# Two encoder layers on one core: Fourier transforms folded twice, value products in runs of six, and roots by Newton steps

## Chip, cores and metric

One core of a Trainium2 chip runs the whole program. The metric is device time in microseconds (us), the median of several runs. The profile comes from one execution that was recorded.

## What is computed

```python
def reference(x, norm1, w_in, w_fourier, b_fourier, q_norm, k_norm, sink, ...):
    for l in range(DEPTH):                       # 2 layers, 512 positions, 1024 channels
        h = rmsnorm(x, norm1[l])
        p = h @ w_in[l]                          # u (512) | q (8 x 64) | k (2 x 64) | v (2 x 64)
        ...
        y_f = fourier_mix(u, w_fourier[l], b_fourier[l])   # Re(FFT2 over positions, channels) @ W_f + b
        q = rope(rmsnorm(q, q_norm[l]))
        k = rope(rmsnorm(k, k_norm[l]))
        y_a = windowed_gqa(q, k, v, sink[l])     # |i-j| <= 128, softmax with a sink
        mix = jnp.concatenate([rmsnorm(y_f, ...), rmsnorm(y_a, ...)], axis=-1)
        x = x + mix @ w_o[l]
        h = rmsnorm(x, norm2[l])
        up = dwconv_centred(h @ w_up[l], conv_w[l], conv_b[l])
        x = x + (jax.nn.silu(gate) * val) @ w_down[l]
    return x
```

All of it is float32 to the outside.

## The kernel before, in words

x lies as eight tiles of 128 channels x 512 positions. A product of matrices is made in one of two ways (`mm3`, L114): plain f32, one matmul instruction that the profile shows as two records on TensorE (L118); or, where both factors were split into a high and a low fp32r part (`split`, L98: ScalarE makes the high part, VectorE the low one), three matmuls high-high, low-high and high-low (L120 to L122). The FFN, q, k, v and W_o go the second way; layer 0's Fourier group goes in plain f32, layer 1's in three fp32r products.

A layer goes as follows. The root of the norm (`col_rstd`, `row_rstd`, `rsqrt`, L206) ends in `rb`, which ScalarE copies (L226). The q, k, v product has two groups: group 1 (q3, k, v) and group 0 (q0 to q2). `fold_h` (L400) multiplies a tile of x by its norm (one SCALAR_TENSOR_TENSOR, "stt") and folds it over positions: `fold` (L329) writes the sum of position n and 512-n (257 columns) and the difference (255 columns), with one COPY of two columns and two TENSOR_TENSOR of 255. The weight W_u is folded over channels in the same way (`fold_wu`, L335). The **u-stage** (L551) multiplies the eight folded tiles by the eight folded weights: for each tile five products of 258 or 256 columns, into three banks `pee` and one `poo`. `stage_out` (L580) and `tail_out` (L570) copy the four blocks (cosine and sine parts of positions and of channels) out of PSUM. Then two DFT **stages** (L594): stage 0 over channels, stage 1 over positions, each thirteen products in plain f32, or 36 matmuls in fp32r, of 256 or 258 columns, against the tables `tabs` and `alts` from `load_tables` (L275). W_f (L620) and its norm follow.

`prep` (L429) makes the roots of q and k (`rsqrt` with n=16 for k and q3, n=24 for q0 to q2) and their rotation. The power itself is one GpSimd instruction (L210, tiles `qk2r`, `qk3r`). `turn_q` and `turn_k` (L473, L483) transpose them on TensorE. `attention` (L500) goes by pairs of heads, 3, 0, 1, 2, in two halves of two query blocks: scores (L517), a reduction on VectorE (L521), the exponential on ScalarE, a scaling on GpSimd (L526), transposes on TensorE (L529), copies on ScalarE (L531), and six value products per half (L536) of 128 rows by 64 columns into the upper or lower half of one bank:

```python
for j in ((0, 1, 2), (1, 2, 3))[half]:
    ...
    for e in range(2):
        nc.tensor.matmul(py[64 * e:64 * e + 64, ...], vp[:, j, ...], pT[:, half, e, ...], ...)
```

The products of W_o's first half are spread between the attention's steps by `issue_after`. W_o's second half and the FFN follow; while layer 0's FFN runs, `presplit` (L149) folds and splits layer 1's weights on ScalarE and VectorE and stores them in DRAM (`kept`).

The order of instructions on each engine is not the code's: the tile framework's scheduler sets it, by its own estimate of when inputs are ready and by free buffers (`TEMPS`, `BANKS`). A change in one place so moves instructions in others.

Of the kernel before, what the change touches and what calls it, by code (L numbers as in the profile page):

```python
# [37 lines left out]
def encoder_kernel(tc, t):  # L38
# [236 lines left out]
    def load_tables(l):  # L275


        rows = t["dft"].rearrange("i p c -> (i p) c")[:, 257:]
        tab = []
        for i in range(2):  # L280
            raw = temp(512, "m4") if l else cp.tile([P, 512], F32, tag=f"th{i}", name=nm("tab"))
            nc.sync.dma_start(raw[:, :257], t["dft"][i, :, :257])
            if i == 0:
                nc.vector.memset(raw[:1, 257:512], 0.0)
                nc.sync.dma_start(raw[1:16, 257:512], rows[:15])
                nc.sync.dma_start(raw[16:, 257:512], rows[15:P - 1])
            else:
                nc.sync.dma_start(raw[:, 257:512], rows[P - 1:2 * P - 1])
            if l:
                tab.append([cp.tile([P, 512], F32R, tag=f"t{z}{i}", name=nm("tab")) for z in "hl"])  # L290
                split(*tab[i], raw)
            else:
                tab.append([raw])
        raw = temp(258, "m4") if l else cp.tile([P, 258], F32, tag="altr", name=nm("altr"))
        nc.vector.memset(raw, 0.0)
        nc.sync.dma_start(raw[:1], t["alt"])
        alt = raw
        if l:
            alt = cp.tile([P, 258], F32R, tag="altr", name=nm("altr"))
            act(alt, raw)  # L300
# [3 lines left out]
        wt = [raw]  # L304
        if l:
            wt = [cp.tile([P, 512], F32R, tag=f"wt{z}", name=nm("wt")) for z in range(2)]
            split(*wt, raw)
        return tab, alt, wt
# [34 lines left out]
    def load_wf(l, j, raw=None):  # L343

        raw = wtile() if raw is None else raw
        nc.sync.dma_start(raw[:, :512].rearrange("p (z c) -> p z c", z=2),
                          t["w_fold"][l, j].rearrange("p (z c) -> p z c", z=2)[:, :, :256])
        return raw

    def fold_wf(raw, w=None):  # L350
# [4 lines left out]
        nc.vector.memset(w[:1, 256:384], 0.0)  # L355
# [12 lines left out]
    for l in range(L):  # L368
# [31 lines left out]
        def fold_h(k):  # L400
            hr = temp(512, "tF")
            stt(hr, x[k], g1[:, l, k:k + 1], rb1, ALU.mult, ALU.mult)
            if l:
                hf = temp(512, "tF")
                fold(hf, hr)
                hs[k] = halves(pair("slab"))
                split(*hs[k], hf)
# [4 lines left out]
            fold(hs[k][0], hr)  # L412
# [86 lines left out]

        def attention(p, first_pair):  # L500
# [5 lines left out]
            for half in range(2):  # L506
                for i in (2 * half, 2 * half + 1):
# [4 lines left out]
                    for e in range(2):  # L512
# [31 lines left out]
        if l == 0:  # L544
            tabs, alts, wt = load_tables(l)
# [7 lines left out]
        for kk in range(KT // 2):  # L553
            if not l:
                wu = load_wu(l, kk)
            for k in (2 * kk, 2 * kk + 1):
# [9 lines left out]
                for m in range(2):  # L566
                    mm3(poo[:, m * 256:(m + 1) * 256], [z[:, 256 + m * P:384 + m * P] for z in h], wo,
                        st and m == 0, sp_, skip_group_check=True)

        def tail_out(pe, scale, turned):  # L570

            b = halves(tp.tile([P, 2, 258], F32R if l else F32, tag="tail", name=nm("tail"), bufs=2))[:1 + l]
            if turned:
# [6 lines left out]
        def stage_out(pe, po, scale, turned=False):  # L580
# [4 lines left out]
            for m in range(2):  # L585
                a = halves(pair("slab")) if l else [two[:, m * 512:(m + 1) * 512]]
                put([z[:, :257] for z in a], pe[m][:, :257], scale)
                put([z[:, 257:] for z in a], po[:, m * 256 + 1:(m + 1) * 256], scale)
                tiles.append(a)
            return tiles, tail_out(pe, scale, turned)  # L590


        ue, ut = stage_out(pee, poo, 1.0, True)
        for stage in range(2):  # L594
            pe = [psum(), psum(), psum("sc")]
            po = psum()
# [239 lines left out]
```

## Time and profile before

| | us |
|---|---|
| median of 3 runs (lowest, highest) | 1065.24 (1064.05, 1065.41) |
| the profiled execution | 1065.23 |
| its span | 1063.4 |
| TensorE busy in the span | 1050.4 (99%) |
| VectorE busy | 722.4 (68%) |
| ScalarE busy | 507.7 (48%) |
| GpSimd busy | 115.6 (11%) |
| granted TensorE clock, mean | 0.998 |

The span reaches from the first to the last recorded instruction; 1.8 us of the profiled execution lie outside it. A record's length is not what it costs: records of one engine overlap (a matmul of 258 columns lasts longer than the distance to the next), so the price of an operation is the distance from its start to the start of the next one on its engine. PE is TensorE, DVE VectorE, ACT ScalarE, POOL GpSimd. A row of a timeline gives the start, the length, the engine, the line, the operation, output and inputs, the count of records that follow each other, and in brackets the idle time before with what ended it.

### The profile page before, as it was taken

Reading aid. Unit: us, or ns where it says so; the run is one execution under the profiler, and the core shown is the slowest. Engines: PE = TensorE matmul, PEld = TensorE weight load, DVE = VectorE, ACT = ScalarE, POOL = GpSimd, SP = SyncE. Lnnn points to the kernel's source line nnn. Section 1 sums busy time; section 2 is a strip of 40 time slices with the busy share of each in tenths; the row PEclk is TensorE's granted clock in tenths of the full one; section 3 lists DMA queues with packets and bytes.
Section 4 is the critical chain, followed back from the end, with each engine's and each line's share of the span. In section 5 each row is a group of like instructions: output and inputs, shape, how many; then the busy total and the mean of one; then the engine's idle time right before and its main releaser. Section 6 shows DMA issues by size and latency. Waiting matters only on the chain.

```text
span 1063.4 us, 14386 instructions
## 1 busy us (share of the span) xinstructions
PE 1050.4 (99%) x5107; PEld 876.5 (82%) x5107; DVE 722.4 (68%) x1340; ACT 507.7 (48%) x939; POOL 115.6 (11%) x168
## 2 busy tenths in 40 slices
PE   8999999999999999999999999999999999999998
PEld 7986778888888888888899877788888888888887
DVE  7868668697766777777519665387887336877632
ACT  5348755455443454455423875155554224544421
POOL 0134410000000000000001542001201000101100
PEclk9999999999999999999999999999999999999999
DMA  8233062233269932339857222422332333232241
GB/s 280 73 109 104 19 197 91 87 99 99 87 206 340 356 96 90 94 112 323 281 182 229 82 78 80 139 82 96 100 99 82 102 114 99 82 104 92 82 148 48
DMA packets 60475, 140.03 MB, mean 132 GB/s; under 512 B 6642, under 2 KB 22258, under 8 KB 60404
## 3 DMA queue, kind: packets, MB, share of 16 engines
q1 hardware_dynamic: 60404, 139.12, 40.3%
q8 instruction: 40, 0.66, 0.2%
q14 instruction: 31, 0.25, 0.1%
HBM read 116.02 MB, written 23.07 MB: 131 GB/s over the span
## 4 chain that ended last, share of the span: by engine, by line
PE 92%; DVE 4%; ACT 1%; POOL 1%; DMA 1%; issue 1%; SPq 0%; DVEq 0%; ACTq 0%; POOLq 0%
PE ps L120 27%; PE ps L121 27%; PE ps L122 27%; PE ps L118 3%; PE ps L536 3%; PE ps L529 2%; PE ps L517 2%; POOL qk3r L210 1%; PE ps L224 1%; DVE act L93 1%; PE ps L217 1%; DVE tF L96 1%; DVE tF L93 0%; DVE slab L93 0%; ACT tA L90 0%
## 5 line engine op out<-in xcount | busy, mean ns | idle before, releaser
L90 ACT ACTIVATE whi<-wraw 128x512 fp32r<-128x512 f32 (+1 forms) x296 | 181.8, 616 | 292.3 <-PE ps L122 275.2
L120 PE MATMUL ps<-act,whi 128*128 128x512 f32 x768 | 298.9, 390 | 0.0
L121 PE MATMUL ps<-act,wlo 128*128 128x512 f32 x768 | 298.7, 389 | 0.0
L122 PE MATMUL ps<-act,whi 128*128 128x512 f32 x768 | 298.4, 389 | 0.0
L93 DVE TENSOR_TENSOR wlo<-wraw,whi 128x512 fp32r<-128x512 f32 (+1 forms) x304 | 219.4, 724 | 100.5 <-ACT whi L90 99.1
L121 PEld LDWEIGHTS ps<-act,wlo 128*128 128x128 f32 x768 | 144.2, 188 | 29.9
L120 PEld LDWEIGHTS ps<-act,whi 128*128 128x128 f32 x768 | 144.2, 188 | 29.9
L122 PEld LDWEIGHTS ps<-act,whi 128*128 128x128 f32 x768 | 144.2, 188 | 29.7
L96 DVE SCALAR_TENSOR_TENSOR tF<-tF,pb,tF 128x511 f32<-128x511 f32 x176 | 133.2, 763 | 10.9 <-ACT tF L90 8.4
L93 DVE TENSOR_TENSOR tF<-ps,rb 128x512 f32<-128x512 f32 x104 | 71.1, 688 | 76.0 <-PE ps L122 64.3
L120 PE MATMUL ps<-slab,whi 128*128 128x512 f32 (+2 forms) x212 | 81.7, 386 | 0.0
L121 PE MATMUL ps<-slab,wlo 128*128 128x512 f32 (+2 forms) x212 | 80.2, 379 | 0.0
L122 PE MATMUL ps<-slab,whi 128*128 128x512 f32 (+2 forms) x212 | 80.0, 382 | 0.0
L90 ACT ACTIVATE tF<-tF,pb 128x512 f32<-128x512 f32 x88 | 71.5, 815 | 9.2 <-DVE tF L93 2.8
L93 DVE TENSOR_TENSOR x<-x,ps 128x512 f32<-128x512 f32 (+1 forms) x49 | 32.9, 673 | 41.0 <-PE ps L122 40.8
L93 POOL TENSOR_TENSOR tF<-tF,tF 128x512 f32<-128x512 f32 x22 | 30.4, 1384 | 255.9 <-DVE tF L96 224.1
L520 POOL COPY tA<-nsink 128x1 f32<-128x1 f32 x64 | 13.4, 216 | 362.3 <-DMA wraw<-in_w_down_dram 317.9
L521 DVE CUSTOM_DVE_ANT_0 tA<-ps,pb,nsink 128x256 f32<-128x256 f32 (+1 forms) x64 | 38.3, 605 | 20.1 <-PE ps L517 15.4
L120 PE MATMUL ps<-pT,whi 128*128 128x512 f32 (+1 forms) x132 | 50.5, 383 | 0.0
L121 PE MATMUL ps<-pT,wlo 128*128 128x512 f32 (+1 forms) x132 | 50.5, 383 | 0.0
L122 PE MATMUL ps<-pT,whi 128*128 128x512 f32 (+1 forms) x132 | 50.5, 383 | 0.0
L122 PEld LDWEIGHTS ps<-slab,whi 128*128 128x128 f32 x212 | 39.6, 188 | 8.4 <-issue 1.2
(170 smaller groups left out, 1545.2 us busy)
## 6 DMA issues: line engine op xcount, KB each, us to landing
wraw<-in_w_up_dram SPq DMA_DIRECT2D x88, 512.0 KB, 3.5
wraw<-in_w_down_dram SPq DMA_DIRECT2D x32, 512.0 KB, 3.6
kept<-tA SPq DMA_DIRECT2D x56, 256.0 KB, 5.5
whi<-kept SPq DMA_DIRECT2D x28, 256.0 KB, 3.0
wlo<-kept SPq DMA_DIRECT2D x28, 256.0 KB, 3.2
kept<-tA SPq DMA_DIRECT2D x32, 192.0 KB, 1.9
wraw<-in_w_down_dram SPq DMA_DIRECT2D x32, 192.0 KB, 2.4
wraw<-in_w_o_dram SPq DMA_DIRECT2D x8, 512.0 KB, 4.1
```

The source lines that it names most:

```text
L90: return nc.scalar.activation(out, in_, func, **kw)
L93: return (eng or nc.vector).tensor_tensor(out, a, b, op=op)
L96: return nc.vector.scalar_tensor_tensor(out=out, in0=a, scalar=s, in1=b, op0=op0, op1=op1)
L118: nc.tensor.matmul(out, a[0], b[0], start=start, stop=stop, **kw)
L120: nc.tensor.matmul(out, a[0], b[0], start=start, stop=False, **kw)
L121: nc.tensor.matmul(out, a[1], b[0], start=False, stop=False, **kw)
L122: nc.tensor.matmul(out, a[0], b[1], start=False, stop=stop, **kw)
L517: nc.tensor.matmul(sc[:, :n], qT[p][:, e, i * P:(i + 1) * P], kT[g][:, s, j0 * P:(j1 + 1) * P], start=s == 0, stop=s == 1)
L520: nc.gpsimd.tensor_copy(pr[:, n:n + 1], nsink[:, l, h:h + 1])
L521: nc.vector.tensor_tensor_reduce(out=pr[:, :n], in0=sc[:, :n], in1=mask[:, m0:m0 + n], scale=qs_scale[p][:, i, e:e + 1], scalar=nsink[:, l ...
L529: tr = nc.tensor.transpose(pp[:, j * P:(j + 1) * P], pr[:, j * P:(j + 1) * P], ident)
L536: nc.tensor.matmul(py[64 * e:64 * e + 64, i0 * P:(i1 + 1) * P], vp[:, j, 64 * g:64 * g + 64], pT[:, half, e, b0:b0 + 2 * (i1 - i0) + 1:2, ...
```

## The change

Four things are changed.

1. **A second fold.** `fold2` splits the even part (257 columns) again, by frequency parity, into 128 and 129 columns, and the odd part into two of about 128. It costs two TENSOR_TENSOR of 2 x 127, two of one column and one COPY of two columns for a tile. It is applied to all eight h tiles in both layers, to layer 0's two tiles that leave the u-stage (the tail there: two TENSOR_TENSOR of 128 behind a copy on ScalarE), and to the eight W_u tiles of layer 1 in `presplit`. In stage 0 each product of 258 or 256 columns becomes one of 130 or 128, their count being the same; in stage 1 the count goes from 13 to 7 (layer 0) and from 36 to 19 (layer 1), each with 258 or 256 columns. The u-stage itself keeps its products. W_f's weights come by four DMAs instead of one (`load_wf`), and y is assembled in four strided pieces instead of two.
2. **Runs of six.** All six value products of a half get a dependency on the last ScalarE copy of that half.
3. **Roots.** For n of 16 and 24, `rsqrt` works on VectorE: a shift and a multiply-add on the integer view, then three Newton steps, eleven small instructions in place of one power on GpSimd. The norm's roots (n=4) stay on GpSimd.
4. **Tables.** They are loaded once, by one DMA and four strided copies on VectorE, and split for layer 1 from that copy.

```diff
 def rsqrt(ssq, n, inv, tag, bufs=2):
     nc.vector.tensor_scalar(v, ssq, inv, EPS, op0=ALU.mult, op1=ALU.add)
-        nc.gpsimd.tensor_tensor(r, v, mhalf[:, :1].to_broadcast([P, n]), op=ALU.pow)
+        if n <= NB:
+            nc.gpsimd.tensor_tensor(r, v, mhalf[:, :1].to_broadcast([P, n]), op=ALU.pow)
+            return r
+        nc.vector.tensor_scalar(it, v.bitcast(I32), 1, None, op0=ALU.logical_shift_right)
+        nc.vector.tensor_scalar(r.bitcast(I32), it, -1, float(0x5F3759DF), op0=ALU.mult, op1=ALU.add)
+        for _ in range(3):
+            tt(q, r, r, ALU.mult)
+            stt(q, q, -0.5, v, ALU.mult, ALU.mult)
+            stt(r, q, 1.5, r, ALU.add, ALU.mult)
...
+    def fold2(dst, src):
+        def two(z, a, n):
+            return z[:, a:a + 2 * n].rearrange("p (a b) -> p a b", a=2)
+        lo, hi = two(src, 0, 256)[:, :, 1:128], two(src, 0, 256)[:, :, 255:128:-1]
+        tt(two(dst, 0, 256)[:, :, 1:128], lo, hi, ALU.subtract)
+        tt(two(dst, 1, 255)[:, :, 128:255], lo, hi, ALU.add)
+        tt(dst[:, 0:1], src[:, 0:1], src[:, 256:257], ALU.subtract)
+        tt(dst[:, 128:129], src[:, 0:1], src[:, 256:257], ALU.add)
+        nc.vector.tensor_copy(dst[:, 256:512:255], src[:, 128:385:256])
...
             stt(hr, x[k], g1[:, l, k:k + 1], rb1, ALU.mult, ALU.mult)
+            hf = temp(512, "tF")
+            fold(hf, hr)
             if l:
-                hf = temp(512, "tF")
-                fold(hf, hr)
+                hg = temp(512, "tF")
+                fold2(hg, hf)
                 hs[k] = halves(pair("slab"))
-                split(*hs[k], hf)
+                split(*hs[k], hg)
                 return
...
-            fold(hs[k][0], hr)
+            fold2(hs[k][0], hf)
...
-                        act(pT[:, half, e, b0:b0 + n // P, :].rearrange("p b q -> p (b q)"), pp[:, :n])
+                        ready = act(pT[:, half, e, b0:b0 + n // P, :].rearrange("p b q -> p (b q)"), pp[:, :n])
...
-                        nc.tensor.matmul(py[64 * e:64 * e + 64, i0 * P:(i1 + 1) * P], vp[:, j, 64 * g:64 * g + 64],
+                        pv = nc.tensor.matmul(py[64 * e:64 * e + 64, i0 * P:(i1 + 1) * P], vp[:, j, 64 * g:64 * g + 64],
...
+                        tc.add_manual_dep(pv.ins, ready.ins.name, both_ready, reason="paired values")
...
+                if stage == 0:
+                    c = slice(m * P, (m + 1) * P)
+                    mm3(pe[m][:, :128], [z[:, c] for z in ue[0]], odd, True, True, skip_group_check=True)
+                    mm3(pe[m][:, 128:258], [z[:, c] for z in ue[1]], even, False, False, skip_group_check=True)
...
+                else:
+                    c = slice(m * P, (m + 1) * P)
+                    mm3(pe[m][:, :258], [z[:, c] for z in tabs], [z[:, :258] for z in ue[min(m, 1)]], True, m == 0)
+                    for z in ut if m else ():
+                        nc.tensor.matmul(pe[m][:, :258], alts[:, :P], z, start=False, stop=z is ut[-1])
```

How this moves instructions shows at three places.

TensorE in layer 0's attention, W_f beside it. `pT` with `v` are the value products (64 x 256 or 64 x 128), `ident` with `tA` the transposes that come before them, `m` with `act` the scores, `slab` or `tail` with `whi` or `wt` W_f. Before:

```order
L529 MATMUL ps_858<-ident,tA_852 128x128 x3
L536 MATMUL ps_803<-pT_808,v_180 64x256
L529 MATMUL ps_878<-ident,tA_872 128x128 x3
L517 MATMUL ps_989<-m_97_550,act_764 128x384 x2
L118 MATMUL ps_1111<-slab_950,whi_1114 128x256 x2
L517 MATMUL ps_1003<-m_97_550,act_764 128x384 x2
L536 MATMUL ps_803<-pT_808,v_180 64x256 x3
L536 MATMUL ps_803<-pT_808,v_180 64x128 x2
L529 MATMUL ps_892<-ident,tA_886 128x128 x3
```

Now:

```order
L118 MATMUL ps_1196<-slab_1030,whi_1202 128x256 x2
L118 MATMUL ps_1222<-slab_1030,whi_1229 128x258 x2
L118 MATMUL ps_1222<-tail_1035,wt_539 128x258
L118 MATMUL ps_1223<-slab_1030,whi_1229 128x256 x2
L565 MATMUL ps_889<-pT_894,v_180 64x256 x4
L565 MATMUL ps_889<-pT_894,v_180 64x128 x2
L558 MATMUL ps_978<-ident,tA_972 128x128 x3
L558 MATMUL ps_992<-ident,tA_986 128x128 x2
```

The six products of a half stood in two or three pieces between other work; now they stand side by side, behind both transposes' copies.

TensorE in the last third of layer 0's u-stage; `whi` is a folded weight, `slab` a pair of folded h tiles, `ps` the bank. Before:

```order
L118 MATMUL ps_589<-whi_641,slab_637 128x258
L118 MATMUL ps_590<-whi_641,slab_637 128x258
L118 MATMUL ps_591<-whi_641,slab_637 128x258
L118 MATMUL ps_592<-whi_641,slab_637 128x256 x2
L118 MATMUL ps_589<-whi_655,slab_637 128x258
L118 MATMUL ps_590<-whi_655,slab_637 128x258
L118 MATMUL ps_591<-whi_655,slab_637 128x258
L118 MATMUL ps_592<-whi_655,slab_637 128x256 x2
```

Now:

```order
L118 MATMUL ps_625<-whi_659,slab_505 128x258
L118 MATMUL ps_624<-whi_682,slab_676 128x258
L118 MATMUL ps_626<-whi_659,slab_505 128x258
L118 MATMUL ps_627<-whi_659,slab_505 128x256 x2
L118 MATMUL ps_625<-whi_682,slab_676 128x258
L118 MATMUL ps_624<-whi_702,slab_676 128x258
L118 MATMUL ps_626<-whi_682,slab_676 128x258
L118 MATMUL ps_627<-whi_682,slab_676 128x256 x2
L118 MATMUL ps_625<-whi_702,slab_676 128x258
L118 MATMUL ps_624<-whi_725,slab_719 128x258
L118 MATMUL ps_626<-whi_702,slab_676 128x258
```

A tile's five products stood together; now products of a tile wait singly, those of the first 128 columns (`ps_624` of `slab_676`) before the older tile's others, since the columns of a tile become ready at different times.

VectorE while the h tiles of layer 0 are folded; `tF` is a tile of h (first its norm, then its first fold), `slab` what the u-stage reads, `whi` with `wraw` a weight's fold, `act` with `ropetab` the rotation, `qk2` and `qk3` the roots. Before:

```order
L331 COPY whi_615<-wraw_613 128x2
L93 TENSOR_TENSOR whi_615<-wraw_613 128x255 x2
L331 COPY whi_624<-wraw_613 128x2
L93 TENSOR_TENSOR whi_624<-wraw_613 128x255 x2
L96 SCALAR_TENSOR_TENSOR tF_681<-x_81,pa,rb_320 128x512
L331 COPY whi_641<-wraw_633 128x2
L93 TENSOR_TENSOR whi_641<-wraw_633 128x255 x2
L331 COPY slab_668<-tF_666 128x2
L93 TENSOR_TENSOR slab_668<-tF_666 128x255 x2
```

Now:

```order
L93 TENSOR_TENSOR whi_1177<-wraw_1172 128x256
L350 COPY slab_676<-tF_672 128x2
L93 TENSOR_TENSOR whi_1177<-wraw_1172 128x256
L96 SCALAR_TENSOR_TENSOR qk2r_550<-qk2q_552,qk2r_550 128x16
L93 TENSOR_TENSOR slab_676<-tF_693 128x2x127
L93 TENSOR_TENSOR slab_719<-tF_715 128x1 x2
L93 TENSOR_TENSOR slab_719<-tF_715 128x2x127
L337 COPY tF_736<-tF_734 128x2
L93 TENSOR_TENSOR tF_736<-tF_734 128x255 x2
L93 TENSOR_TENSOR act_808<-act_808 128x512
L216 TENSOR_SCALAR qk3r_812<-qk3i_815 128x24
```

A tile's way into `slab` was one COPY and two folds of 255; now those go into another `tF` and four more instructions and a COPY follow, with pieces of other tiles, of the roots and of W_f's folds (128x256) between them.

## Rows read from the trace of the kernel before

**Rows 1.** The page: last chain by engine, ScalarE's largest group, one kind of load.
```profile
PE 92%; DVE 4%; ACT 1%; POOL 1%; DMA 1%; issue 1%; SPq 0%; DVEq 0%; ACTq 0%; POOLq 0%
...
L90 ACT ACTIVATE whi<-wraw 128x512 fp32r<-128x512 f32 (+1 forms) x296 | 181.8, 616 | 292.3 <-PE ps L122 275.2
...
wraw<-in_w_o_dram SPq DMA_DIRECT2D x8, 512.0 KB, 4.1
```

**Rows 2.** Timeline of TensorE, layer 0: u-stage, stage 0, first transposes, first scores.
```profile
46.20 4.17 PE L118 MATMUL ps<-whi,slab 128*128 128x258 f32 x18
...
63.66 1.90 PE L118 MATMUL ps<-tab,slab 128*128 128x258 f32 x8
...
69.30 0.60 PE L490 MATMUL ps<-ident,m 128*128 128x128 f32 x4
...
79.13 0.49 PE L517 MATMUL ps<-m,m 128*128 128x256 f32 x2
```

**Rows 3.** Timeline of VectorE, layer 0, from `rb` to the root of q0 to q2.
```profile
29.75 4.06 DVE L96 SCALAR_TENSOR_TENSOR tF<-x,pa,rb 128x512 f32<-128x512 f32 x6 [4.27 <-ACT rb L90]
33.73 0.16 DVE L331 COPY slab<-tF 128x2 f32<-128x2 f32 x1
33.80 0.75 DVE L93 TENSOR_TENSOR slab<-tF 128x255 f32<-128x255 f32 x2
34.47 0.16 DVE L331 COPY slab<-tF 128x2 f32<-128x2 f32 x1
...
50.30 1.26 DVE L438 TENSOR_REDUCE qkssq<-act 128x8 f32<-128x512 f32 x2
...
67.02 0.18 DVE L443 TENSOR_SCALAR qknr<-qk3r 128x24 f32<-128x24 f32 x1 [2.56 <-POOL qk3r L210]
```

**Rows 4.** Timeline of VectorE, layer 1: the same stretch, its start and its wait.
```profile
558.16 0.75 DVE L96 SCALAR_TENSOR_TENSOR tF<-x,pa,rb 128x512 f32<-128x512 f32 x1 [11.58 <-ACT rb L90]
...
593.57 0.18 DVE L443 TENSOR_SCALAR qknr<-qk3r 128x24 f32<-128x24 f32 x1 [3.38 <-POOL qk3r L210]
```

**Rows 5.** Timeline of TensorE, layer 1: end of the u-stage, stage 0, first scores.
```profile
588.35 1.04 PE L490 MATMUL ps<-ident,m 128*128 128x128 f32 x8
589.14 0.36 PE L120 MATMUL ps<-tab,slab 128*128 128x258 f32 x1
...
590.74 0.28 PE L121 MATMUL ps<-tab,slab 128*128 128x258 f32 x1
590.86 0.28 PE L122 MATMUL ps<-tab,slab 128*128 128x258 f32 x1
...
597.34 0.41 PE L517 MATMUL ps<-m,m 128*128 128x256 f32 x2
```

**Rows 6.** The chain of waits, value products: start, us of the chain, count of records.
```profile
91.44 0.58 PE ps L536 x2
...
109.22 1.23 PE ps L536 x12
```

**Rows 7.** Timeline of TensorE, layer 1's last run of value products and its neighbours.
```profile
668.77 0.40 PE L122 MATMUL ps<-slab,whi 128*128 128x512 f32 x1
669.00 0.39 PE L120 MATMUL ps<-slab,whi 128*128 128x512 f32 x1
669.32 1.08 PE L536 MATMUL ps<-pT,v 128*64 128x256 f32 x6
670.33 0.50 PE L121 MATMUL ps<-slab,wlo 128*128 128x512 f32 x1
670.67 0.40 PE L122 MATMUL ps<-slab,whi 128*128 128x512 f32 x1
```

**Rows 8.** Stretches: length, busy time of PE, PEld, DVE, ACT, POOL, granted clock, DMA share, GB/s.
```profile
25.00:30.00 5.00, 3.35 (x15) 3.35 (x16) 0.73 (x3) 3.09 (x9) 1.03 (x1) 0.73 0.36 140
85.00:90.00 5.00, 3.77 (x22) 2.70 (x21) 2.68 (x13) 5.00 (x17) 2.96 (x8) 1.00 0.27 84
340.00:350.00 10.00, 10.00 (x46) 8.29 (x45) 9.51 (x24) 4.63 (x10) 0.00 (x0) 1.00 0.92 312
```

More of the change, by code (lines that the diff above doesn't have):

```diff
@@ L273, in encoder_kernel, with load_tables, load_last @@
     nc.vector.tensor_scalar(nsink, sink, -1.0, None, op0=ALU.mult)
[L275 to L300, printed above, removed]
+    def load_tables():
+        raw = wtile()[:, :512]
+        nc.sync.dma_start(raw, t["dft"][0])
+        tab = cp.tile([P, 512], F32, tag="tab", name="tab")
+        for c0, c1, r0 in ((0, 128, 1), (128, 257, 0), (257, 384, 258), (384, 512, 257)):
+            nc.vector.tensor_copy(tab[:, c0:c1], raw[:, r0:r0 + 2 * (c1 - c0) - 1:2])
+        alt = cp.tile([P, 258], F32, tag="alt", name="alt")
+        nc.vector.memset(alt, 0.0)
+        nc.sync.dma_start(alt[:1], t["alt"])
+        return [tab], alt, load_last(0)
+    def load_last(l):
         raw = temp(512, "m4") if l else cp.tile([P, 512], F32, tag="wt0", name=nm("wt"))
@@ L303, in load_tables, with split_tables @@
         nc.sync.dma_start(raw[:1], t["w_fourier"][l, 256:257, :])
[L304 to L308, printed above, removed]
+        return raw
+    def split_tables(tab, alt):
+        parts = []
+        for n, src in ((512, tab[0]), (512, load_last(1))):
+            tag = "tw"[len(parts)]
+            parts.append([cp.tile([P, n], F32R, tag=("wt" if tag == "w" else "tab") + z, name=nm("parts")) for z in "01"])
+            split(*parts[-1], src)
+        alr = cp.tile([P, 258], F32R, tag="altr", name="altr")
+        act(alr, alt)
+        return parts[0], alr, parts[1]
     def add_square(acc, src, first, tag="sq"):
@@ L333, in fold @@
         tt(dst[..., 257:512], src[..., 1:256], src[..., 511:256:-1], ALU.subtract)
-    def fold_wu(raw, w=None):
-        w = temp(512, "tA") if w is None else w
-        fold(w, raw)
+    def fold2(dst, src):
[7 more added lines that the diff above has]
+        nc.vector.tensor_copy(dst[:, 256:512:255], src[:, 128:385:256])
+    def fold_wu(raw, w=None):
+        if w is not None:
+            fold(w, raw)
+            return w
+        one, w = temp(512, "tA"), temp(512, "tA")
+        fold(one, raw)
+        fold2(w, one)
         return w
@@ L586, in stage_out @@
                 a = halves(pair("slab")) if l else [two[:, m * 512:(m + 1) * 512]]
-                put([z[:, :257] for z in a], pe[m][:, :257], scale)
-                put([z[:, 257:] for z in a], po[:, m * 256 + 1:(m + 1) * 256], scale)
+                o = [temp(512, "tF")] if first and not l else a
+                put([z[:, :257] for z in o], pe[m][:, :257], scale)
+                put([z[:, 257:] for z in o], po[:, m * 256 + 1:(m + 1) * 256], scale)
+                if o is not a:
+                    fold2(a[0], o[0])
                 tiles.append(a)
-            return tiles, tail_out(pe, scale, turned)
+            return tiles, tail_out(pe, scale, first)
         ue, ut = stage_out(pee, poo, 1.0, True)
+        even, odd = [z[:, 128:258] for z in tabs], [z[:, :128] for z in tabs]
+        sines = [[z[:, 256 + i * P:384 + i * P] for z in tabs] for i in range(2)]
         for stage in range(2):
@@ new lines, in encoder_kernel @@
+            for m in range(2):
+                if stage == 0:
+                    c0 = (257, 384)[m]
+                    for i in range(2):
+                        mm3(po[:, m * 256 + i * P:m * 256 + (i + 1) * P], [z[:, c0:c0 + P] for z in ue[i]], sines[i],
+                            m == 0 and i == 0, m == 1 and i == 1, skip_group_check=True)
+                else:
+                    mm3(po[:, m * 256:(m + 1) * 256], sines[m], [z[:, 256:512] for z in ue[m]],
+                        m == 0, m == 1, skip_group_check=True)
```

57 lines of the change are left out of this document (31 added, 26 removed).

## The prediction, made before the changed kernel ran

> **What bounds the kernel now.** I read the page's last chain first: 92% of it is TensorE's own work [rows 1]. So a product removed is worth its price, unless the engine that feeds TensorE takes its place. The change loads VectorE, so the stretches to read are those where VectorE feeds TensorE: the two Fourier groups. In layer 0 TensorE starts the u-stage at 46.20, stage 0 at 63.66, k's transposes at 69.30 and the first score at 79.13; the 80 u-stage records go at 17.46 / 80 = 0.218 us each without a hole, 0.436 a product [rows 2]. VectorE starts its tiles at 29.75, when `rb` is there, and has no gap until it runs out at 67.02 - 2.56 = 64.46, waiting for GpSimd's root [rows 3]. So before, VectorE finishes its last fold just ahead of the products that read it. Layer 1 is alike: VectorE starts at 558.16, then waits 3.38 for the root until 593.57 [rows 4], while the u-stage ends at 588.35 and the first score comes at 597.34 [rows 5]. Little slack stands between the two engines.
>
> **Prices, start to start.** VectorE [rows 3]: stt of 512 columns (33.73 - 29.75) / 6 = 0.66; the COPY 0.07; a TENSOR_TENSOR of 255 columns 0.335; so a fold 0.74. Other operations of 512 columns 0.60 (the two reductions last 1.26 with their overlap), of 384 by the line between those 0.47, of 256 0.335; an instruction of 16 or 24 columns lasts 0.18 against the COPY's 0.16, so 0.08. The second fold has no row: two TENSOR_TENSOR of 254 elements at 0.335, two of one column and one COPY at 0.07, together 0.88 (dearer, by strided reading, is a rival below; cheaper than its columns has no reason). TensorE: an fp32r product of 258 columns 0.12 and a transpose of 128 columns 0.79 / 8 = 0.10 [rows 5].
>
> An fp32r product of **128 columns** has no row. Below, half of the 258-column price, 0.06; above, half of the plain f32 product, 0.22 [rows 2]. I take 0.11, nearest to the transposes.
>
> **Layer 0, Fourier group.** The table's split stands ahead of `rb`'s copy on ScalarE, so VectorE starts about 0.6 later (616 ns each [rows 1]), at 30.4. The table's load also takes a buffer in `load_wu`'s turn, so W_u's second load waits for group 0's last weights; a load of 512 KB lands 4.1 after its issue [rows 1], and about 4 us of folds stand on VectorE meanwhile: 0 to 1, taken 0. Up to the last piece of the eighth h tile its queue now holds 8 stt 5.3, 8 folds 5.9, 8 second folds 7.0, 8 weight folds 5.9, 3 splits of 384 1.4, 5 reductions 3.0, 8 operations of 512 4.8, 8 half-rotations 2.7, W_f's folds 1.5 and 14 small ones 1.1: 38.6, so 69.0. The tiles come one by one, and the products behind them: tile 4's last piece comes at about 63.8, and behind it stand 17 products, 7.4, and 0.8 of waiting, so the u-stage ends at about **72.0** instead of 63.66, with TensorE idle between tiles. Behind that VectorE still has 9 us, k's rotation, splits, Newton steps and the second fold of the u-stage's two output tiles, mixed: the last input of stage 0 is there at 78.2. On the way to the first score then lie stage 0 at half columns and half of k's transposes 3.7, five products of stage 1 2.2, q3's eight transposes 0.9, six products of W_f 2.6, together 9.4: the first score at 87.7, **+8.6**. The cuts in stage 0 (13 x 0.22 = 2.8) are in this, and 0.43 of stage 1's six products (2.6) falls behind the first score.
>
> **Values.** Their products stand in 42 runs, the first at 91.44, the last at 669.32. Twelve records (six products) in one run take 1.23, two take 0.58 [rows 6], six 1.01. Around a run the neighbours lose 0.32 - 0.23 = 0.09 on entry and 0.34 - 0.23 = 0.1 on exit [rows 7]; over all runs 0.17 each. 30.3 in the runs and 7.1 around them, 37.4 in all, against 16 runs x (1.23 + 0.17) = 22.4: **-15**, of it 6.2 in layer 0 and 8.7 in layer 1. The wait for the last copy costs nothing where other products stand ahead, which the order shows (W_f or W_o between). So layer 0 ends its first half of W_o at +8.6 - 6.2 - 0.4 = +2.0. [...] One such drop in layer 0's holes: **+3.4** in all.
>
> **Layer 1.** From 558.16 the queue holds 37.7 up to the last split of the eighth tile (8 second folds 7.0, 8 stt 5.3, 8 folds 5.9, 8 low parts 4.8, 5 reductions 3.0, 11 of 512 6.6, 10 half-rotations 3.35, 21 small 1.7): 595.9, and 11 products behind it: u-stage end 597.2 against 588.35, **+8.9**. From there to the first score it took 8.99 [rows 5]; GpSimd's hold of VectorE, 3.38 [rows 4], goes, of which the splits behind it need about 1.4 again, and 36 products at 0.11 for 0.12 give 0.4, so 6.6 to 6.7: first score 603.9, +6.6 (at 0.06 a product +4.8, at 0.22 +10.5). Then stage 1 has 17 matmuls fewer, -2.0, and values -8.7: -4.1, and a shorter clock drop +1.0: **-3.1** (from -4.9 to +0.8).
>
> **FFN.** `presplit` has 8 more second folds, 7 us of VectorE. Where it folds, VectorE is busy for 9.51 of 10 us, TensorE for 10.00 [rows 8]; the cover is thin, so 0 to 2, taken 0.5. The DMAs of W_f (four for one) and of the tables (fewer) run far ahead of use: nothing, with the queue's lead as cover.
>
> **Sum.** +3.4 - 3.1 + 0.5 = +0.8: on the profiled 1065.23, which is the median's 1065.24 too, **1066**. About 23 us of TensorE's work goes and about as much comes back as holes in front of it.
>
> **Rivals.**
> - *Second folds are dear (slower).* If each of their two long instructions holds VectorE for its whole record (255 columns: 0.75 - 0.335 = 0.415 [rows 3]) and the three small ones for 0.16 each, a second fold takes 1.31, 0.43 more, eight times in a layer, in front of the same products: 2 x 3.5 more, 1073. The rows speak against it, since the next instruction starts after 0.335; for it, that two strides in one operand have no row. Chance 0.05. [...]
> - *128 columns are dear (slower).* At 0.22 a product stage 0 of layer 1 costs 36 x 0.11 = 4 more: 1070. It decides from 0.15 upward. For it: plain f32 pays 0.218 a record; against it: transposes at 0.10. Chance 0.18.
> - *The clock stays low through the piecemeal u-stages (slower).* TensorE would run about 9 us in each layer at half pace: 2 x 4 more, 1074. It decides if the holes of 2 to 3 us between tiles lower the clock as the one of 2 us did [rows 8]. Chance 0.13.
> - *Waits in the attention go too (faster).* Around 85 to 90 TensorE is busy for only 3.77 of 5 [rows 8], and GpSimd's roots, 9 us each, stand ahead of its other work there. If q's earlier roots and the six in a run let these holes close, 2 x 2.5: 1060. Against it: the queue of VectorE, not the root, is last now. Chance 0.22.
> - *VectorE holds less than counted (faster).* If the holes take other products, stage 0 and the transposes, the u-stages end 4 us later instead of 8.5, and the result is about 1055. Against it: the order shows no other product in the holes. Chance 0.08.
> - *The runs of six come apart.* The order shows them contiguous; chance 0.01.
>
> **Numbers.** My forecast has 0.33, with a range of its own from 1061 to 1071. A measurement can tell about 0.2%, 2.1 us, here from no change, so "same" is 1063.1 to 1067.4. The forecast's own 0.33 splits into 0.08, 0.19 and 0.06 (its range, cut at these two). Faster: 0.22 + 0.08 + 0.08 = 0.38. Same: 0.19, and 0.01 from the last rival: 0.20. Slower: 0.06 + 0.18 + 0.13 + 0.05 = 0.42. The range that leaves 2 in 10 out reaches from the two faster cases to the two slower: 1054 to 1075.
>
> **What would show it.** In the new profile: the u-stages end at about 72 and 597, with idle TensorE inside and VectorE unbroken up to 69 and 596; the first scores at about 88 and 604; value records in groups of twelve at about 1.23; no GpSimd record of 9 us; the last product of stage 0 of layer 1 about 0.11 apart. I am wrong if TensorE shows no holes in the u-stages (then near 1050), or if VectorE's rows for the second fold are clearly longer than 0.335.

## The result, and the profile after

| | us | to before |
|---|---|---|
| before, median of 6 | 1065.18 (1064.05 to 1065.68) | |
| changed, median of 6 | 1068.31 (1067.91 to 1069.43) | ratio 1.0033, 95% interval 1.0020 to 1.0046 |
| the changed kernel's profiled execution | 1068.19, span 1066.4, mean granted clock 0.989 | |

The change is slower by 3.1 us. TensorE does 11.6 us less and the program still ends later. One of the four executions of e4 (below) took 2101.66 us, for a reason that is not known, and e4's median is that of the other three. The page of the changed kernel (busy time, share, instructions; the chain by engine), to be read against [rows 1]:

```profile
PE 1038.8 (97%) x5078; PEld 872.6 (82%) x5078; DVE 748.1 (70%) x1533; ACT 503.0 (47%) x937; POOL 89.7 (8%) x164
...
PE 89%; DVE 7%; ACT 2%; issue 1%; DMA 0%; POOL 0%; ACTq 0%; DVEq 0%
```

VectorE's part of the last chain grew from 4% to 7%: it now stands between TensorE's pieces. Where, the timeline of TensorE in layer 0 shows, which answers to [rows 2]: the u-stage has three holes of about 2 us, stage 0 (L118 with `tab`) has two more, and the first score (L546) starts at 89.11 instead of 79.13.

```profile
46.54 7.64 PE L118 MATMUL ps<-whi,slab 128*128 128x258 f32 x34
56.54 2.53 PE L118 MATMUL ps<-whi,slab 128*128 128x258 f32 x8 [2.35 <-DVE slab L93]
60.59 2.09 PE L118 MATMUL ps<-whi,slab 128*128 128x258 f32 x4 [1.52 <-DVE slab L93]
64.92 9.25 PE L118 MATMUL ps<-whi,slab 128*128 128x258 f32 x34 [2.24 <-DVE slab L350]
75.78 0.82 PE L118 MATMUL ps<-tab,slab 128*128 128x128 f32 x4 [1.61 <-DVE slab L93]
...
77.84 0.46 PE L118 MATMUL ps<-tab,slab 128*128 128x128 f32 x2 [1.01 <-DVE slab L93]
...
89.11 0.82 PE L546 MATMUL ps<-m,m 128*128 128x256 f32 x4
```

VectorE's timeline of the same stretch, against [rows 3]. It starts on the tiles at 30.73 (after the table's copies and split, which wait for a DMA and for ScalarE), the last piece of tile 4 (L350 at 64.69) releases TensorE at 64.92, the last piece of the eighth tile starts at 70.02, and the last input of stage 0 at 80.74. Two long instructions of the second fold take 77.95 - 77.28 = 0.67.

```profile
27.24 0.63 DVE L294 COPY tab<-wraw 128x128 f32<-128x128 f32 x4 [1.41 <-DMA wraw<-in_dft_dram]
30.12 0.69 DVE L93 TENSOR_TENSOR parts<-tab,parts 128x512 fp32r<-128x512 f32 x1 [2.25 <-ACT parts L90]
30.73 0.74 DVE L96 SCALAR_TENSOR_TENSOR tF<-x,pa,rb 128x512 f32<-128x512 f32 x1
...
64.69 0.17 DVE L350 COPY slab<-tF 128x2 f32<-128x2 f32 x1
...
70.02 0.09 DVE L350 COPY slab<-tF 128x2 f32<-128x2 f32 x1
...
77.28 0.74 DVE L93 TENSOR_TENSOR slab<-tF 128x254 f32<-128x254 f32 x2
77.95 0.16 DVE L470 TENSOR_SCALAR qknr<-qk3r 128x24 f32<-128x24 f32 x1
...
80.74 0.16 DVE L350 COPY slab<-tF 128x2 f32<-128x2 f32 x1
```

The stretches (length, busy PE, PEld, DVE, ACT, POOL, granted clock, DMA share, GB/s), against [rows 8]: VectorE is full, TensorE busy for 1.23 to 2.53 of 5 us in three of the five, and its granted clock is 0.50 in the stretch of 60 to 65.

```profile
55.00:60.00 5.00, 2.53 (x8) 1.50 (x8) 5.00 (x20) 0.00 (x0) 0.00 (x0) 0.80 0.19 54
60.00:65.00 5.00, 2.17 (x5) 1.26 (x5) 5.00 (x18) 0.00 (x0) 0.00 (x0) 0.50 0.18 52
65.00:70.00 5.00, 5.00 (x16) 4.14 (x17) 5.00 (x27) 0.00 (x0) 0.00 (x0) 0.68 0.18 52
585.00:590.00 5.00, 1.23 (x4) 0.93 (x4) 5.00 (x18) 0.63 (x1) 0.00 (x0) 0.70 0.73 253
590.00:595.00 5.00, 4.38 (x24) 4.38 (x25) 5.00 (x24) 0.76 (x2) 0.00 (x0) 0.61 0.16 35
```

Layer 1 on TensorE, against [rows 5]: the same holes, products of 258 columns 0.22 apart (591.00 to 591.22; the granted clock from 591 to 592 was 0.50) where they were 0.12 apart, products of 128 columns 0.11 apart (606.59 to 606.70; the clock from 605 to 607 was 1.00), and the first score at 607.87.

```profile
587.31 1.23 PE L120 MATMUL ps<-whi,slab 128*128 128x258 f32 x4 [2.48 <-ACT slab L90]
590.62 0.58 PE L121 MATMUL ps<-whi,slab 128*128 128x258 f32 x1 [2.09 <-DVE slab L93]
591.00 0.42 PE L122 MATMUL ps<-wlo,slab 128*128 128x258 f32 x1
591.22 0.42 PE L121 MATMUL ps<-whi,slab 128*128 128x258 f32 x1
...
606.59 0.28 PE L121 MATMUL ps<-parts,slab 128*128 128x128 f32 x1
606.70 0.28 PE L122 MATMUL ps<-parts,slab 128*128 128x128 f32 x1
...
607.87 0.48 PE L546 MATMUL ps<-m,m 128*128 128x256 f32 x2
```

And the values, against [rows 6]: a half in one run, 104.73 to 105.97.

```profile
104.73 1.30 PE L565 MATMUL ps<-pT,v 128*64 128x256 f32 x12
105.97 0.76 PE L558 MATMUL ps<-ident,tA 128*128 128x128 f32 x5
```

Five starts on TensorE divide the program: the first score of layer 0, the first product of the attention's norm behind W_o's first half (L217, now L227), the product of layer 1's first norm (the same line), and again layer 1's first score and the end of its W_o half. They serve for all kernels below (us; "after first score" is from there to the end of W_o's first half).

| | layer 0: first score | after it | FFN | layer 1: norm to first score | after it |
|---|---|---|---|---|---|
| before | 79.13 | 78.25 | 387.97 | 51.99 | 80.84 |
| changed | 89.11 | 72.09 | 387.21 | 59.46 | 73.76 |
| difference | +10.0 | -6.2 | -0.8 | +7.5 | -7.1 |

The differences come to +3.4; behind the last start, to the end of the span, the changed kernel takes 0.4 less. The starts are not clean borders. In layer 0, 17 matmuls of W_o's second half stand ahead of the attention's norm in the changed kernel, and 14 in the kernel before. These three take 0.7 us, so like for like the stretch after the first score shrinks by 6.9 and the FFN by 0.1.

### The profile page after: what moved, and what is told of

It is laid out like the page before. It is cut to its first block, busy times and chain, and to the rows that moved or that the text cites. A ratio compares the mean times of both kernels' runs of the same rounds, so it can differ in the third digit from the quotient of the medians.

```text
span 1066.4 us, 14524 instructions
## 1 busy us (share of the span) xinstructions
PE 1038.8 (97%) x5078; PEld 872.6 (82%) x5078; DVE 748.1 (70%) x1533; ACT 503.0 (47%) x937; POOL 89.7 (8%) x164
## 4 chain that ended last, share of the span: by engine, by line
PE 89%; DVE 7%; ACT 2%; issue 1%; DMA 0%; POOL 0%; ACTq 0%; DVEq 0%
PE ps L122 27%; PE ps L120 27%; PE ps L121 27%; DVE act L93 1%; PE ps L565 1%; PE ps L558 1%; PE ps L118 1%; PE ps L546 1%; DVE tF L93 1%; DVE tF L96 1%; PE ps L234 1%; DVE slab L93 1%; ACT tA L90 1%; DVE tA L550 1%; PE ps L227 1%
## 5 line engine op out<-in xcount | busy, mean ns | idle before, releaser
L96 DVE SCALAR_TENSOR_TENSOR tF<-tF,pb,tF 128x511 f32<-128x511 f32 x176 | 133.5, 763 | 10.6 <-ACT tF L90 8.0
L555 POOL TENSOR_SCALAR tA<-tA,den 128x256 f32<-128x256 f32 (+1 forms) x64 | 37.7, 595 | 156.9 <-DVE den L554 155.9
```

The costliest lines, as they stand in the source:

```text
L96: return nc.vector.scalar_tensor_tensor(out=out, in0=a, scalar=s, in1=b, op0=op0, op1=op1)
L555: nc.gpsimd.tensor_scalar(pr[:, :n], pr[:, :n], den[:, i:i + 1], 1.0, op0=ALU.mult, op1=ALU.mult)
```

## Experiments

All times to the kernel before on the same chip in the same runs; intervals are 95%.

| kernel | median us | difference | ratio |
|---|---|---|---|
| e1 runs of six alone | 1053.37 | -11.7 | 0.9892 [0.9876, 0.9909] |
| e2 roots alone | 1070.34 | +5.3 | 1.0044 [1.0029, 1.0059] |
| e3 runs and roots | 1057.32 | -7.7 | 0.9923 [0.9908, 0.9938] |
| e4 changed, no second fold of h | 1054.78 | -10.2 | 0.9906 [0.9890, 0.9923] |
| e5 changed, roots on GpSimd | 1064.96 | -0.1 | 1.0000 [0.9991, 1.0009] |
| e6 runs, root of 24 columns alone | 1053.32 | -11.8 | 0.9884 [0.9869, 0.9899] |
| e7 channels' second fold alone | 1050.34 | -14.7 | 0.9858 [0.9843, 0.9873] |
| e8 changed, h's second fold on GpSimd | 1072.27 | +7.2 | 1.0083 [1.0052, 1.0114] |
| e9 e7 and root of 24 columns | 1047.82 | -17.6 | 0.9834 [0.9819, 0.9849] |
| e10 changed, root of 16 columns on GpSimd | 1063.57 | -1.8 | 0.9982 [0.9972, 0.9991] |
| e11 changed, no runs of six | 1079.89 | +14.5 | 1.0132 [1.0115, 1.0149] |

### The parts alone: e1, e2, e3

e1 has the dependency of the values and nothing else:

```diff
-                        act(pT[:, half, e, ...], pp[:, :n])
+                        ready = act(pT[:, half, e, ...], pp[:, :n])
...
+                        tc.add_manual_dep(pv.ins, ready.ins.name, both_ready, reason="paired values")
```

> The kernel before with the runs of six alone (all six value products of a half wait for the half's last copy). Theory (the runs' saving reaches the end, the rest of the change gives it back): the value records take 10.6 us less in the changed kernel's two attentions, and the neighbours of the 26 runs that disappear up to 4 us less: 1065.2 - 10.6 - (0 to 4) = 1051 to 1055. Rival (waiting for the last copy opens new holes in the attention as large as the saving): 1061 or more.

Measured 1053.37, within the theory. The first scores stay (78.74, and 51.99 after layer 1's norm); the stretches behind them shrink from 78.25 to 74.15 and from 80.84 to 74.08.

e2 has the Newton steps and nothing else:

```diff
-        nc.gpsimd.tensor_tensor(r, v, mhalf[:, :1].to_broadcast([P, n]), op=ALU.pow)
+        if n <= NB:
+            nc.gpsimd.tensor_tensor(r, v, mhalf[:, :1].to_broadcast([P, n]), op=ALU.pow)
+            return r
...
+        for _ in range(3):
+            tt(q, r, r, ALU.mult)
+            stt(q, q, -0.5, v, ALU.mult, ALU.mult)
+            stt(r, q, 1.5, r, ALU.add, ALU.mult)
```

> The kernel before with the roots of q and k on VectorE alone. Theory: GpSimd's hold of VectorE (2.6 in layer 0, 3.4 in layer 1) goes, 22 small instructions of 0.08 come (1.8 a layer), and VectorE's folds still end in time: between -3 and +0.5, 1062 to 1066. Rival (the roots' chain of small dependent instructions on VectorE delays the folds of the u-stage): 1067 or more.

Measured 1070.34: the rival's range, but not by its mechanism. The u-stage's end does not move; the first score of layer 1 comes 55.86 after the norm instead of 51.99, and layer 0 ends 2.8 later. In the kernel before, GpSimd makes k's root in 3.35, and VectorE goes on with k at 573.05 (timelines of GpSimd and VectorE in layer 1):

```profile
568.52 3.35 POOL L210 TENSOR_TENSOR qk2r<-qk2v,mhalf 128x16 f32<-128x16 f32 x1 [20.85 <-DVE qk2v L209]
```

```profile
573.05 0.16 DVE L443 TENSOR_SCALAR qknr<-qk2r 128x16 f32<-128x16 f32 x1
573.13 0.68 DVE L93 TENSOR_TENSOR act<-pT,qk2r 128x512 f32<-128x512 f32 x1
```

In e2 the steps stand one by one in VectorE's queue, between other tiles' work, from before 573.84 to 591.31, and k goes on at 591.90. Counted from the layer's norm (545.36 before, 547.50 in e2) that is 44.4 instead of 27.7, some 17 us later:

```profile
573.84 0.17 DVE L216 TENSOR_SCALAR qk2r<-qk2i 128x16 int32<-128x16 int32 x1
...
588.07 0.17 DVE L93 TENSOR_TENSOR qk2q<-qk2r 128x16 f32<-128x16 f32 x1
590.04 0.43 DVE L96 SCALAR_TENSOR_TENSOR slab<-ps,slab 128x257 fp32r<-128x257 f32 x1 [1.80 <-ACT slab L90]
...
591.31 0.17 DVE L96 SCALAR_TENSOR_TENSOR qk2r<-qk2q,qk2r 128x16 f32<-128x16 f32 x1
...
591.90 0.68 DVE L93 TENSOR_TENSOR act<-pT,qk2r 128x512 f32<-128x512 f32 x1
```

Eleven instructions, each 0.09 us from its start to the next one's (591.31 to 591.40), became a delay of 17 us. k's rotation, split and transposes then come behind the u-stage, on the way to the first score.

e3 is e1 and e2 together.

> The kernel before with the runs of six and the roots on VectorE, no second fold, old tables. Theory (parts add up): e1 and e2 together, 1050 to 1055, so that the second fold with its tables costs 13 to 18 us of the changed kernel's 1068.3. Rival (the roots are what delays the u-stage): 1060 or more.

Measured 1057.32, between the two ranges: -11.7 and +5.3 make -6.4, and -7.7 was found. The parts nearly add up. What is left of the change, second folds and tables, then costs 3.1 + 7.7 = 10.8 us.

### The second fold of h: e4 and e8

```diff
             if l:
-                hg = temp(512, "tF")
-                fold2(hg, hf)
...
-                split(*hs[k], hg)
+                split(*hs[k], hf)
...
-            fold2(hs[k][0], hf)
+            fold(hs[k][0], hr)
```

> The changed kernel with the second fold of the eight h tiles left out in both layers: the u-stage reads the first fold, so the Fourier output is not the reference's; TensorE's work is unchanged, VectorE has 7 us less ahead of each u-stage. Theory (VectorE's second folds of h are what holds TensorE): both u-stages end about where they did before (64 to 65, and 588 to 590 of layer 1's time), the clock stays full, and 1068.3 - 15 to 18 = 1050 to 1053. Rival 1 (the table's load, the later loads of W_u or the roots' chain hold the u-stage): 1060 or more, with holes left in the u-stage. Rival 2 (the holes themselves are cheap and the low clock is the price): the same end, but the granted clock between 50 and 80 stays under 0.95.

Measured 1054.78, 13.4 less than the changed kernel, by the differences to before. Both u-stages run without a hole: layer 0's starts its last record at 63.20 (before 63.44), and layer 1's comes 42.8 after the norm (before 42.9). TensorE's u-stage of layer 0 in e4:

```profile
45.95 17.62 PE L118 MATMUL ps<-whi,slab 128*128 128x258 f32 x80
```

From 45 to 85 the granted clock is 1.00, so rival 2, as it was put, falls for layer 0; in layer 1 the clock still falls once, to 0.66 from 590 to 595. Holes and low clock went together, so their shares are not told apart. h's second folds cost 6.7 a layer (5.6 and 5.9 by the profiled executions, e4's being the longest of its three), nearly the 7.0 that were counted for them on VectorE. The gain was less than the theory's 15 to 18: without them the late k still holds the first score (55.00 after layer 1's norm).

e8 keeps h's second folds and gives their two long instructions to GpSimd (`fold2(hg, hf, nc.gpsimd)`).

> The changed kernel with the two long instructions of h's second fold on GpSimd instead of VectorE (the one of one column and the COPY stay). Theory (VectorE's load ahead of the u-stages is the price, 12.6 us by e4): VectorE has 0.67 less a tile, 5.4 a layer; GpSimd takes 1.38 us for 512 columns, so about 0.7 each, 11 us a layer within a stretch of 35: 1068.3 - 4 to 10 = 1058 to 1064. Rival (GpSimd's latency takes the place, or it slows VectorE beside it): 1067 or more.

Measured 1072.27, slower than the changed kernel by 4.1: the rival, by its second reason, that GpSimd slows VectorE beside it. Groups on GpSimd in e8 (count, busy us, mean ns):

```profile
L93 POOL TENSOR_TENSOR slab<-tF 128x254 f32<-128x254 f32 x16 | 23.0, 1438 | 21.7 <-DVE tF L93 15.9 <-DVE slab L350 2.8 <-DVE qk2i L215 2.4
L93 POOL TENSOR_TENSOR tF<-tF 128x254 f32<-128x254 f32 x16 | 19.9, 1246 | 27.7 <-DVE tF L93 19.0 <-DVE qk3r L216 4.4 <-DVE qk2i L215 2.8
```

A record lasts 1.25 to 1.44 in the mean, where 0.7 was expected, but about half of that is waiting: the two engines took turns. One place shows it (timelines of GpSimd and VectorE in e8):

```profile
61.31 1.17 POOL L93 TENSOR_TENSOR slab<-tF 128x254 f32<-128x254 f32 x1 [2.53 <-DVE tF L93]
```

```profile
61.15 0.74 DVE L96 SCALAR_TENSOR_TENSOR tF<-x,pa,rb 128x512 f32<-128x512 f32 x1
61.81 0.70 DVE L209 TENSOR_SCALAR qk3v<-qkssq 128x24 f32<-128x24 f32 x1
62.43 0.41 DVE L93 TENSOR_TENSOR act<-pT,ropetab 128x256 f32<-128x256 f32 x1
```

VectorE's first instruction ends at 61.89. GpSimd's ends 0.59 later, at 62.48, and VectorE's instruction of 24 columns, which lasts about 0.17 elsewhere, ends with it, at 62.51. So it goes with nearly all of the 32 records. They last 0.73 to 3.08, yet 29 of them end 0.58 to 0.61 after an instruction of VectorE has ended; in 27 the next one of VectorE ends 0.01 to 0.04 behind GpSimd's, and in the other five it lasts some 0.5 longer than usual. GpSimd's own work is then about 0.6, and VectorE stands still for some 0.5 of it, more than the 0.335 that the instruction takes on VectorE itself. Instructions of VectorE that do not meet such an end keep their length: the weight's folds of 255 columns last 0.411 in the mean from 30 to 73 in e8, and 0.419 in the changed kernel.

The theory that VectorE's load is the price is not touched by this; moving the load took nothing off VectorE, whose busy time is 752.9 in e8 and 748.1 in the changed kernel.

### The roots within the changed kernel: e5, e10, e6

e5 is the changed kernel with all roots of q and k on GpSimd, as before.

> The changed kernel with the roots of q and k back on GpSimd. In the runs so far k's root is ready 15 to 19 us later on VectorE than on GpSimd, since its Newton steps stand one by one between the tiles' folds. Theory (the roots cost about 4 to 5 us here as they do without the second fold, e2 and e3): 1068.3 - 3 to 6 = 1062 to 1065. Rival (here the second folds end last anyway, so the roots are hidden): 1067 to 1069; or GpSimd's 9.4 us for q's root now end last: 1069 or more.

Measured 1064.96, as the theory: the roots cost 3.3 of the changed kernel. All of it is in layer 0 (first score 83.67 instead of 89.11, 73.99 after it instead of 72.09); layer 1 as a whole, from its norm to the end of W_o's first half, takes 133.22 in both. With k's root early, k's transposes (L507) and q3's (L496) go between the late tiles, and the u-stage ends later (78.8) but the first score earlier. The timeline of TensorE in e5:

```profile
66.23 1.11 PE L507 MATMUL ps<-ident,m 128*128 128x128 f32 x4 [2.40 <-ACT m L90]
67.14 4.41 PE L118 MATMUL ps<-whi,slab 128*128 128x258 f32 x10
71.38 1.04 PE L507 MATMUL ps<-ident,m 128*128 128x128 f32 x8
...
77.48 1.47 PE L118 MATMUL ps<-whi,slab 128*128 128x258 f32 x6
...
83.67 0.48 PE L536 MATMUL ps<-m,m 128*128 128x256 f32 x2
```

e10 puts only the root of 16 columns (k and q3) back: `if n <= NB` becomes `if n <= 16`.

> The changed kernel with k's and q3's root back on GpSimd, q0 to q2's on VectorE. Theory (of the roots' 3.3 us in e5 the late root of k is the larger part; q's root on GpSimd for 9.4 us costs or saves under 1.5): 1064 to 1066. Rival (VectorE's queue is so long that any root in it is late): 1067 or more.

Measured 1063.57, a little under the theory's range: the late root of k and q3 costs 4.9, and the root of q0 to q2 on VectorE gains 1.7 beside e5, of it 133.2 - 131.9 = 1.3 in layer 1. e6 has that root alone on VectorE, with the runs of six, in the kernel before (e3 with the same one line changed).

> Runs of six, and only the root of q0 to q2 (24 columns, the one that took 9.4 us on GpSimd) on VectorE; k's and q3's root stays on GpSimd. Theory (the loss of e2 and e3 comes from k's late root, since k's rotation and transposes stand before the first score): within 1 us of the runs of six alone, 1052.5 to 1054.5, or a little under. Rival (q's root, 2 to 4 us later on VectorE than before, is what costs): 1056 to 1058, as e3.

Measured 1053.32, as e1: the theory. Layer 1's first score comes 50.35 after the norm instead of 51.99.

### The runs within the changed kernel: e11

e11 takes the line with `add_manual_dep` out of the changed kernel.

> The changed kernel without the runs of six: the products of a half go again when their own copy is there. Theory (the part is independent of the others: 11.7 us in e1, 13.0 between e2 and e3): 1068.3 + 10 to 13 = 1078 to 1081. Rival (in the changed kernel the first score is so late that the attention has less other work to spread, and the runs bring less): 1070 to 1076.

Measured 1079.89, 11.4 more by the differences: the theory. The runs bring the same with and without the rest.

### What pays, alone: e7 and e9

Stage 0 sums over positions and stage 1 over channels (the kernel in words has them the other way round), so the second fold of h shortens stage 0, and that of the channels stage 1. e7 keeps the second fold of the channels (W_u of layer 1 in `presplit`, the u-stage's output in layer 0), the runs of six and the halved stage 1. h is folded once; stage 0 goes with the old two tables; the roots are on GpSimd.

```diff
-            fold2(hs[k][0], hf)
+            fold(hs[k][0], hr)
...
-                    mm3(pe[m][:, :128], [z[:, c] for z in ue[0]], odd, True, True, skip_group_check=True)
-                    mm3(pe[m][:, 128:258], [z[:, c] for z in ue[1]], even, False, False, skip_group_check=True)
+                    for i in range(2):
+                        mm3(pe[m][:, :258], [z[:, c] for z in ue[i]], [z[:, 0:258] for z in ptabs[i]], i == 0, False)
...
-            for c0, v0, n, k in ((0, 128, 128, 1), (129, 1, 127, 2)):
...
+            tt(y[:, 1:256], u[:, 1:256], pv[:, 1:256], ALU.subtract)
+            tt(y[:, 511:256:-1], u[:, 1:256], pv[:, 1:256], ALU.add)
```

> Runs of six, roots on GpSimd, and the second fold over channels alone (on the weights of layer 1, and on layer 0's output of the u-stage), none on the eight h tiles: stage 1 keeps its half of the products, stage 0 is as before. Theory (a fold pays where VectorE is not ahead of TensorE): stage 1's 2.6 and 2.0 us of TensorE go, 1 to 3 us come back for layer 0's second folds behind the u-stage: 1053.4 - 1.5 to 4 = 1049 to 1052. Rival (these folds, too, stand on the way to the first score and give all of it back): 1053 to 1056.

Measured 1050.34, the theory. Layer 0's u-stage is one piece again (timeline of TensorE in e7), and the end of its W_o half comes 2.4 earlier than in e1 (150.45 against 152.89 from the start), nearly the 2.6 that stage 1 lost. In layer 1 almost nothing came: 125.82 from the layer's norm to the end of W_o's first half against 126.07 in e1, though stage 1 takes 1.9 less there.

```profile
44.62 17.62 PE L118 MATMUL ps<-whi,slab 128*128 128x258 f32 x80
```

e9 adds the root of q0 to q2 on VectorE (`if n <= 16`).

> e7 (second fold over channels alone, runs of six) with the root of q0 to q2 on VectorE, k's and q3's on GpSimd. In e6 that root brought 1.6 us in layer 1 (first score 50.35 instead of 51.99 after the layer's norm) and nothing in layer 0. Theory (GpSimd's 9.4 us still end last in layer 1 of e7): 1050.3 - 1 to 2 = 1048.3 to 1049.3. Rival (in e7 the attention's own chain ends last, as it took the 1.9 us that stage 1 gave up there): 1050 to 1051.

Measured 1047.82, a little better than the theory's range: 17.6 us under the kernel before, and the best of all versions tried. Its page:

```profile
PE 1031.6 (99%) x5078; PEld 868.7 (83%) x5078; DVE 735.2 (70%) x1423; ACT 506.1 (48%) x939; POOL 97.8 (9%) x166
```

TensorE has 18.8 us less work than before and the end moves by 17.6. In the changed kernel it had 11.6 less, at a lower clock (0.989 in the mean, 1.000 in e9), and the end moved the other way.

## Why the prediction came out as it did

The time lies in the range, 2.3 us above the forecast of 1066, and on the side that had the largest chance, slower, though the forecast itself stood inside "same". The sum forecast +0.8 and +3.1 was measured. That it came so near is in part luck: layer 1 missed by +3.5 and layer 0 by +0.4, the FFN by -1.3, and the 0.4 saved behind the last start stands in no term.

- **Layer 0, right in the sum.** Forecast: last piece of tile 4 at 63.8, of the eighth tile at 69.0, end of the u-stage at 72.0, last input of stage 0 at 78.2, first score at 87.7 (89.1 with the clock's 1.4), sum of the layer +3.4. Measured: 64.69, 70.02, 74.2, 80.74, 89.11, and 161.20 against 157.38 at the end of W_o's half, +3.8 (+3.1 like for like). VectorE started 0.3 later than forecast (30.73 for 30.4) and lost some tenths more by the way. The last input came 2.5 late, but from it to the first score it took 8.4 and not 9.4, since part of stage 0 ran before it. Behind the first score the runs of six bring 5.1 of the 6.2 counted there (72.09 against e11's 76.45, and the three matmuls' 0.7), and the rest of that stretch shrinks by 1.8 (e11 against before, 78.25) where 0.4 was counted: two misses that cancel.
- **The second fold's price, right.** 0.335 for a long instruction was taken, 0.67 for two was measured; e4 puts all of h's second folds at 13.4. The rival of dear folds (1073) falls with that: the record lasts 0.415 in the mean (layer 0 of the changed kernel, 16 of them), and the next one starts after 0.335.
- **128 columns, right.** 0.11 was taken between 0.06 and 0.22; the rows show 0.11. The rival (1070) falls. In layer 1, then, halving the columns of stage 0 saved next to nothing (36 products, 0.01 each), for the 7 us counted on VectorE.
- **Clock, half right.** One drop of 1.4 in layer 0, which is 0.27 x 5 from the clock of 0.73 in [rows 8], and one of 1.0 in layer 1 were taken. No run shows either as a loss of time apart from the holes. In the kernel before, by stretches of 1 us, the clock was 0.63, 0.50, 0.50 and 0.67 from 27 to 31. In the changed kernel's Fourier groups it was low twice in layer 0 (0.80, 0.50 and 0.68 from 55 to 70, and 0.84 and 0.81 from 75 to 85) and once in layer 1 (0.70 and 0.61 from 585 to 595). On the path, 17 products behind tile 4 took 9.25 where 7.4 and 0.8 of waiting were forecast, 1 us more. The rival of a clock that stays low throughout (1074) falls.
- **Layer 1, wrong by 3.5.** The step that failed is "Then stage 1 has 17 matmuls fewer, -2.0, and values -8.7". The first score was nearly where forecast (+7.5 for +6.6), but the stretch behind it shrank by 7.1 instead of 10.7. e1 has the values alone, and there this stretch shrinks by 6.8; the value records themselves take 6.0 less in the changed kernel (15.9 to 9.9, start to start), so of the 2.5 that the neighbours were to gain some 0.8 came. Most of the rest turned into waits: TensorE is busy 8.0 less in this stretch of e1, and idle for 2.4 where it was 1.1 (length, busy PE, PEld, DVE, ACT, POOL, granted clock, DMA share, GB/s; before, then e1):

```profile
597.34:678.18 80.84, 79.75 (x489) 61.47 (x488) 46.11 (x145) 48.33 (x134) 23.84 (x59) 1.00 0.25 79
```

```profile
592.17:666.25 74.08, 71.73 (x490) 59.85 (x489) 46.56 (x145) 48.03 (x134) 24.43 (x59) 1.00 0.28 86
```

  Stage 1's 1.9 brings 0.2 in e7 (73.84 against e1's 74.08), and in e11, which has no runs of six, the stretch is 0.6 shorter than before (80.27). In the changed kernel TensorE is idle for 2.4 of it too, and its scores take 0.7 us more than before, start to start. Work that fills gaps of the attention isn't worth its price there.
- **Values, mis-sized.** -15 was forecast for both layers, e1 and e11 measure -11.7 and -11.4. The 10.6 in the records came; of the 4.4 around them about 1 did.
- **Roots, mis-sized.** They were counted as small instructions on VectorE (eleven of 0.08 ahead of the u-stage's end, 0.9 in a layer) and as the end of GpSimd's hold (-2.0 in layer 1), about nothing in all. They cost 3.3 us of the changed kernel (e5), and 5.3 alone (e2). The root of k and q3 does it: put back alone it gains 4.9 (e10). From the norm, k's root comes 17 us later in e2's layer 1 than before, and 21 later in the changed kernel (46.75) than in e5 (25.76). The order was at hand to show where each step stood; the sum of VectorE's queue took that into the first score's time, but no rival asked what the kernel would be with the roots left where they were.
- **FFN, mis-sized.** 0.5 was taken, and the table has -0.8. Of that, 0.7 is the three matmuls of W_o that stand ahead of the norm; they do so in e1 and e2 too, where `presplit` is untouched and the stretch takes 387.29. Like for like the FFN moved by 0.1: the 7 us counted for `presplit` on VectorE cost TensorE nothing.
- **The faster rivals.** The attention's waits stayed (0.66 and 0.5 before 614 and at 111 in the changed kernel), and no other product filled the holes; e5 shows that k's transposes would have, had k's root been early.

So the account of the change, from the runs: the runs of six -11.4 to -11.7; h's second folds +13.4; roots +3.3; the rest, second folds over channels and tables, by e3 and e4 -2.5 (e7 against e1: -3.1). These come to +2.5 to +2.8, and +3.1 was measured. The new tables were not tried alone, nor k's root without q3's.

## What to carry to other kernels

A fold that halves products moves work from one engine to another, and in these runs it paid only where the products did not already wait for the engine that folds: the second fold gained 2.4 us behind the u-stage of layer 0, next to nothing (0.2) where it was done beforehand for layer 1, and lost 13.4 where VectorE was full. A short chain of dependent instructions in VectorE's full queue cost here not its length but its number of turns, as the scheduler sets them: k's root was ready 14 to 21 us earlier by one instruction of 3.35 us on GpSimd than by eleven of 0.09 us. When one change holds several parts, cost each by what it does to the next start on the critical engine, and try them apart: here one part of -11.7 was hidden under two others.

## What was not expected of the hardware

In e8 VectorE and GpSimd took turns: 29 of 32 f32 TENSOR_TENSOR of 254 elements on GpSimd ended 0.58 to 0.61 us after an instruction of VectorE, whether their record lasted 0.73 or 2.55, and VectorE's instructions of 1 to 24 columns that met such an end lasted up to 0.71 in place of about 0.16. A record's length on GpSimd thus held the wait for VectorE as well. An fp32r product of 128 or 130 columns started 0.11 after the one before (606.59 to 606.70 in the changed kernel), where 256 and 258 columns took 0.12 (590.74 to 590.86 in the kernel before): half the columns gained 0.01 per product.
